# A 15-product matmul kernel: transposes in strict order with buffers per row, another product scheme, and divided block sums

## The chip, the cores and the metric

The kernel runs on one core of one Trainium2 chip. The metric is the device time of one execution in microseconds (us); lower is better. A run that is over 1.5% above the fastest run of the same kernel is called slow.

The engines are named as the profile names them: PE is TensorE, PEld its weight loads, DVE is VectorE, ACT is ScalarE, POOL is GpSimd, and SPq is the queue of SyncE, which here issues transposes, stores, weight loads and the first four x loads.

## The reference

```python
def setup_inputs():
    batch, m, k, n = 16, 512, 1024, 768
    return {"x": randn(batch, m, k), "w1": randn(k, n), "w2": randn(k, n)}   # float32

def reference(x, w1, w2):
    y1 = np.matmul(x, w1)
    y2 = np.matmul(x, w2)
    return (np.tanh(y1) * y2).astype(np.float32)
```

The 8192 rows of x are 64 row tiles of 128.

## The kernel before

Tiles 0 to 5 (the head) and tile 63 (the tail) are multiplied plainly. The 57 between form 19 triples. A triple is a block product of 3 row tiles x 2 halves of K with 2 halves of K x 3 column blocks. It would need 18 block products; a bilinear scheme does it in 15. Left operands are sums of x blocks (`A_SUMS`, ten small adds per triple, on VectorE or GpSimd), right operands are sums of weight blocks, made once (`B_SUMS`). Results are put together by letting products accumulate in PSUM banks, with copies and adds between them (`C_OPS`): "p" is a product of 4 matmuls of 128 x 512, "copy" and "seed" are ScalarE copies, "add" is VectorE, "t"/"th" are tanh of a full or half width, "m"/"mh" the multiplies by the second result. Names that begin with c are PSUM banks, those with s are SBUF tiles. In the cuts below, ... marks what is left out, and the comments behind # are mine.

```python
C_OPS = (
    ...
    ("p6", "p", (), "c1", 15, 40, True),
    ("add263", "add", ("copy327", "p6"), "c2", "c1", "s327", (-1, 1)),
    ("p12", "p", ("add263",), "c2", 47, 44, False),
    ...
    ("add16", "add", ("copy63", "p4"), "s16", "c6", "s63", (1, 1)),      # to SBUF
    ("m1", "m", ("add16", "t1"), 1, "s16", 1),                           # multiply: two SBUF inputs
    ...
    ("add38", "add", ("add128", "add16", "copy39", "p4"), "c6", "c6", "s39", (-1, 1)),
    ("p5", "p", ("add128", "add16", "add38"), "c6", 13, 43, False),
    ...
    ("add32", "add", ("copy7", "p0"), "s32", "c6", "s7", (1, 1)),        # to SBUF
    ("th1", "th", ("add32",), 1, "s32", 1),
    ("mh1", "mh", ("add32", "th1"), 1, "s32", 1),                        # half multiply: two SBUF inputs
)
PE_ORDER = "10 4+ 7 2+ 6 9 13+ 12 8 5+ 11 3 1+ 0+ 14+"     # "+": done in the next triple's period
```

The program is laid out by a list scheduler on the host (`Planner`). It is given each operation's engines, duration and dependencies ("needs" and "behind" become waits on the chip, "issued" is order in the program only), picks an engine and a place for each, and the instructions are then emitted in that order. Each engine's list keeps that order, and a wait in it holds up what stands behind: in the trace of the kernel before, VectorE sat 2.23 us at one sum with an add behind it that TensorE was waiting for (253.48 us, in the prediction). So a number in the planner changes no instruction's speed, but can change what stands behind what. A row tile comes in as follows:

```python
def load_x(e, mt):                       # GpSimd issues; f32 in HBM becomes f16 in SBUF
    xhs[mt] = xhpool.tile([P, K], f16, tag="xh", name="xh")
    pin(nc.gpsimd.dma_start(xhs[mt], xf[mt]))

def transpose(e, mt):                    # the SyncE queue issues
    xts[mt] = xtpool.tile([P, KO, P], f16, tag="xT", name="xT")
    pin(nc.sync.dma_start_transpose(xts[mt], xhs[mt]))
...
    op(f"L{mt}", {"pool": 0.55}, None, [], load_x, mt, issued=[prev] + ..., behind=..., xfer=1.38)
    op(f"T{mt}", {"sp": 0.05}, None, [f"L{mt}"], transpose, mt,
       behind=xt_readers[mt - XT_BUFS] if mt >= XT_BUFS else [], xfer=1.2)
```

## Time and profile before

| | before |
|---|---|
| median of the three runs ahead of the prediction | 335.29 us (334.16 to 336.82) |
| the profiled run | 339.59 us, span of the profile 337.8 us |
| work of the 19 triples at full pace | 19 x 60 matmuls x 0.2158 = 246.0 us |

The profiled run was slower than all three timed ones, 1.6% over the fastest. From the page of the kernel before, the busy shares and two rows of the span in 40 slices (a digit is the busy share in tenths, for PEclk the granted clock):

```profile
PE 299.8 (89%) x1394; PEld 138.1 (41%) x1394; DVE 246.9 (73%) x407; ACT 216.3 (64%) x430; POOL 149.2 (44%) x161
...
PE   7799949996999999999898898979797879899992
...
PEclk9999996997999999999999999999999999999998
```

The row of PE shows a dip in slice 6 and one in slice 10 (counted from 1), the clock falls in slices 7 and 10, and the pattern is broken from slice 20 on.

To compare kernels I use one figure throughout: in a stretch that holds only 128 x 512 matmuls, time lost = its length - (number of matmuls) x 0.2158 us. The count comes from the view of busy time by stretches. For the kernel before, 40 us from 90 hold 187 matmuls (nothing lost), and 150 us from 130 hold 599, so 150 - 129.3 = 20.7 us are lost.

### The profile page before, as it was taken

How to read it: one execution, taken by the hardware profiler on the slowest of the kernel's cores; microseconds unless marked ns; L12 is line 12 of the kernel's file. 1: busy time of each engine (PE TensorE's matmuls, PEld its weight loads, DVE VectorE, ACT ScalarE, POOL GpSimd, SP SyncE). 2: the span in 40 equal slices, each digit the busy share in tenths (PEclk: the TensorE clock that was granted, in tenths of full speed). 3: DMA queues.
4: the chain of work that ended last, by engine and by line, in shares of the span. 5: the costliest groups of instructions: out<-in, count | busy, mean ns of one | idle time of the engine just before them, and what ended most of it. 6: DMA issues, size and time to landing. Idle time of an engine off the chain costs nothing.

```text
span 337.8 us, 4563 instructions
## 1 busy us (share of the span) xinstructions
PE 299.8 (89%) x1394; PEld 138.1 (41%) x1394; DVE 246.9 (73%) x407; ACT 216.3 (64%) x430; POOL 149.2 (44%) x161
## 2 busy tenths in 40 slices
PE   7799949996999999999898898979797879899992
PEld 5456413442444444434343343434343334344440
DVE  0349997979679787887768687767768588898562
ACT  4595945884898876756676564757575565854531
POOL 2003274484367363663827365462718175451000
PEclk9999996997999999999999999999999999999998
DMA  8999999979999999799897999989897979533034
GB/s 266 340 406 192 194 171 322 230 124 217 185 218 245 155 228 230 129 230 134 223 197 163 210 143 241 108 222 121 232 157 186 172 169 265 98 142 140 0 143 188
DMA packets 84122, 65.33 MB, mean 193 GB/s; under 512 B 65664, under 2 KB 65664, under 8 KB 84096
## 3 DMA queue, kind: packets, MB, share of 16 engines
q1 hardware_dynamic: 74880, 47.72, 58.1%
q0 software_dynamic: 8640, 15.73, 30.5%
q10 hardware_dynamic: 576, 1.57, 1.2%
q8 instruction: 11, 0.18, 0.3%
q14 instruction: 15, 0.12, 0.1%
HBM read 39.85 MB, written 25.17 MB: 192 GB/s over the span
## 4 chain that ended last, share of the span: by engine, by line

## 5 line engine op out<-in xcount | busy, mean ns | idle before, releaser
L421 PE MATMUL bank<-b,s 128*128 128x512 f16 x608 | 144.8, 382 | 26.9 <-DVE bank L436 18.9
L421 PEld LDWEIGHTS <-s 128*128 128x128 f16 x760 | 74.9, 99 | 122.4 <-issue 37.3
L439 ACT ACTIVATE o<-s 128x512 f32<-128x512 f32 (+1 forms) x57 | 31.8, 558 | 68.7 <-DVE s L436 68.7
L380 POOL TENSOR_TENSOR s<-xT,s 128x512 f16<-128x512 f16 x37 | 43.0, 1164 | 64.1 <-PE bank L421 61.9
L380 POOL TENSOR_TENSOR s<-xT 128x512 f16<-128x512 f16 x35 | 42.3, 1226 | 53.6 <-DMA xT<-xh 28.0
L336 ACT ACTIVATE junk<-xh 128x1024 f16<-128x1024 f16 x60 | 63.1, 1052 | 0.9 <-DMA xh<-in_x_dram 0.7
L427 ACT ACTIVATE s<-bank 128x512 f32<-128x512 f32 x95 | 55.9, 589 | 9.5 <-PE bank L421 9.5
L421 PEld LDWEIGHTS <-xT 128*128 128x128 f16 x380 | 37.2, 98 | 45.3 <-issue 0.8
L436 DVE TENSOR_TENSOR bank<-s,bank 128x512 f32<-128x512 f32 x76 | 52.2, 687 | 4.3 <-PE bank L421 3.6
L444 DVE TENSOR_TENSOR o<-o,bank 128x512 f32<-128x512 f32 (+1 forms) x76 | 40.3, 548 | 17.6 <-PE bank L421 11.2
L421 PE MATMUL bank<-b,xT 128*128 128x512 f16 x228 | 52.5, 379 | 0.0
L436 DVE TENSOR_TENSOR s<-bank,s 128x512 f32<-128x512 f32 x57 | 38.8, 685 | 5.0 <-PE bank L421 3.5
L394 PE MATMUL bank<-wh,xT 128*128 128x512 f16 (+1 forms) x200 | 39.3, 353 | 1.3 <-DVE wh L312 0.7
L421 PE MATMUL bank<-wh,s 128*128 128x512 f16 x152 | 39.9, 386 | 0.0
L421 PE MATMUL bank<-wh,xT 128*128 128x512 f16 x152 | 38.8, 379 | 0.0
L329 POOL DMA_DIRECT2D xh<-in_x_dram x60 | 33.7, 563 | 7.4 <-DMA xT<-xh 3.9
L444 DVE TENSOR_TENSOR o<-o,s 128x512 f32<-128x512 f32 (+1 forms) x38 | 35.5, 934 | 0.5 <-ACT o L439 0.5
L439 ACT ACTIVATE o<-bank 128x256 f32<-128x256 f32 (+1 forms) x57 | 24.2, 453 | 17.0 <-DVE s L436 11.0
L380 DVE TENSOR_TENSOR s<-xT 128x512 f16<-128x512 f16 x22 | 16.4, 747 | 21.2 <-DMA xT<-xh 16.2
L380 POOL TENSOR_TENSOR s<-s,xT 128x512 f16<-128x512 f16 x19 | 27.6, 1453 | 8.8 <-DVE s L380 8.8
L380 DVE TENSOR_TENSOR s<-s,xT 128x512 f16<-128x512 f16 x38 | 20.4, 536 | 11.8 <-PE bank L421 10.4
L394 PEld LDWEIGHTS <-xT 128*128 128x128 f16 x200 | 19.6, 99 | 19.5 <-issue 2.1
(41 smaller groups left out, 149.0 us busy)
## 6 DMA issues: line engine op xcount, KB each, us to landing
out_dram<-o SPq DMA_DIRECT2D x63, 384.0 KB, 3.6
xh<-in_x_dram POOLq DMA_DIRECT2D x60, 256.0 KB, 5.6
w_f<-in_w_dram SPq DMA_DIRECT2D x12, 384.0 KB, 9.0
x_f<-in_x_dram SPq DMA_DIRECT2D x4, 512.0 KB, 8.2
w_f<-in_w_dram ACTq DMA_DIRECT2D x4, 384.0 KB, 9.1
xT<-xh SPq DMA_TRANSPOSE x60, 5.8
out_dram<-o_last SPq DMA_DIRECT2D x1, 384.0 KB, 4.7
```

The lines of the kernel that those rows point to most:

```text
L329: pin(nc.gpsimd.dma_start(xhs[mt], xf[mt]))
L336: pin(nc.scalar.activation(junk[:, :src.shape[-1]], src, ACT.Abs, scale=scale, accum_out=sums[:, column:column + 1]))
L380: pin(engine[e].tensor_tensor(ss[i, v], x_operand(i, a), x_operand(i, b), OP[how]))
L394: pin(nc.tensor.matmul(b, xts[mt][:, k, :], rhs, start=first, stop=k == KO - 1, skip_group_check=True))
L421: pin(nc.tensor.matmul(place(i, dst), x_operand(i, a)[:, k, :], w_rhs(b, k), start=begins and k == 0, stop=k == KH - 1, skip_group_check=T ...
L427: pin(nc.scalar.activation(d, place(i, src), ACT.Copy, scale=float(sign)))
L436: pin(nc.vector.tensor_tensor(d, a, b, ALU.add if signs == (1, 1) else ALU.subtract))
L439: pin(nc.scalar.activation(out_tile(HEAD + 3 * i + r)[:, lo:lo + n], place(i, src)[:, :n], ACT.Tanh, scale=float(sign)))
L444: pin(nc.vector.tensor_tensor(o, o, place(i, src)[:, at:at + n], ALU.mult))
```

## The change

The intent, in five parts: (1) each transpose is issued only after the one of the row tile ahead of it, and transposed tiles get four buffers for each of a triple's three rows (12, were 10 in one ring), with more xh (6, were 5) and output buffers (4 of each, were 3) and longer transpose latencies in the planner; (2) another 15-product scheme in which every multiply reads its second result from a PSUM bank, and so does every tanh but two per triple; (3) with it, another order of the products; (4) a fixed division of x block sums, five on GpSimd and five on VectorE; (5) at the start, GpSimd's x loads wait for a weight slice (the gate, empty before), and the head's stores go later. Two planner entries of the check at the end (f1, f4) changed as well.

```diff
-    (5, 1, 4, "add"), (13, 5, 8, "add"), (20, 16, 4, "sub"), ...
+    (10, 2, 8, "sub"), (3, 1, 2, "add"), (34, 32, 2, "sub"), ...
+ON_POOL = (34, 35, 51, 10, 21)
 ...                                   (B_SUMS and C_OPS replaced; some lines of the new C_OPS:)
+    ("p6", "p", (), "c3", 15, 5, True),
+    ("add312", "add", ("copy376", "p6"), "c5", "c3", "s376", (1, 1)),
+    ("p9", "p", ("add312",), "c5", 31, 37, False),
+    ("add2", "add", ("copy63", "p1"), "c2", "c1", "s63", (1, 1)),
+    ("m0", "m", ("add2", "t0"), 0, "c2", 1),
+    ("add4", "add", ("copy56", "p3"), "c8", "c1", "s56", (-1, 1)),
+    ("th0", "th", ("add4",), 0, "c8", 1),
+    ("mh0", "mh", ("add4", "th0"), 0, "c8", 1),
 ...
-PE_ORDER = "10 4+ 7 2+ 6 9 13+ 12 8 5+ 11 3 1+ 0+ 14+"
+PE_ORDER = "7 0+ 13+ 6 10 4+ 5+ 9 12 1 14 3+ 2+ 11 8"
 ...                                   (planner: an operation may name its own latency; slack of 1.0 for transfers "behind")
-    XH_BUFS, XT_BUFS, S_BUFS, O_BUFS, C_BUFS, WF_BUFS = 5, 10, 2, 3, 2, 8
+    XH_BUFS, XT_BUFS, S_BUFS, O_BUFS, C_BUFS, WF_BUFS = 6, 4, 2, 4, 2, 8
-        xts[mt] = xtpool.tile([P, KO, P], f16, tag="xT", name="xT")
+        xts[mt] = xtpool.tile([P, KO, P], f16, tag=f"xT{mt % 3}", name="xT")
-    def nothing(e):
-        pass
+    def gate(e):
+        pin(nc.gpsimd.tensor_copy(held, wfs[1, GATE][:, :1]))
-            op(f"S{v}.{i}", {"dve": 0.416, "pool": 1.2}, ...
+            op(f"S{v}.{i}", {"pool": 1.25} if v in ON_POOL else {"dve": 0.45}, ...
-           issued=[f"T{HEAD + 5}"] if mt < HEAD else [], xfer=1.0)
+           issued=[f"T{HEAD + 8 + mt // 3 * 3}"] if mt < HEAD else [], xfer=1.0)
         op(f"T{mt}", {"sp": 0.05}, None, [f"L{mt}"], transpose, mt,
-           behind=xt_readers[mt - XT_BUFS] if mt >= XT_BUFS else [], xfer=1.2)
+           issued=[f"T{mt - 1}"] if mt > 4 else [],
+           behind=xt_readers[mt - 3 * XT_BUFS] if mt >= 3 * XT_BUFS else [], xfer=1.2, latency=3.0)
```

More of the change, by code (lines that the diff above doesn't have):

```diff
@@ L15 @@
 A_SUMS = (
-    (5, 1, 4, "add"), (13, 5, 8, "add"), (20, 16, 4, "sub"), (12, 4, 8, "add"), (28, 12, 16, "sub"),
-    (15, 2, 13, "add"), (60, 32, 28, "sub"), (47, 15, 32, "sub"), (42, 47, 5, "sub"), (63, 16, 47, "sub"),
+    (10, 2, 8, "sub"), (3, 1, 2, "add"), (34, 32, 2, "sub"), (35, 34, 1, "sub"), (11, 3, 8, "sub"),
+    (51, 16, 35, "add"), (15, 11, 4, "sub"), (31, 16, 15, "sub"), (63, 31, 32, "add"), (21, 10, 31, "add"),
 )
 B_SUMS = (
-    (48, 32, 16, "sub"), (40, 8, 32, "sub"), (3, 1, 2, "sub"), (6, 2, 4, "sub"), (43, 3, 40, "sub"),
@@ L21 @@
-    (44, 4, 40, "add"), (45, 6, 43, "add"), (18, 16, 2, "sub"), (19, 1, 18, "add"), (36, 44, 8, "sub"),
-    (27, 8, 19, "sub"),
+    (48, 32, 16, "sub"), (5, 1, 4, "add"), (36, 32, 4, "sub"), (6, 4, 2, "sub"), (37, 1, 36, "sub"),
+    (24, 8, 16, "add"), (45, 37, 8, "sub"), (18, 16, 2, "sub"), (29, 5, 24, "sub"), (27, 29, 6, "sub"),
+    (26, 2, 24, "sub"),
 )
+ON_POOL = (34, 35, 51, 10, 21)
 C_OPS = (
     ("p10", "p", (), "c0", 32, 8, True),
-    ("copy327", "copy", ("p10",), "s327", "c0", 1),
@@ L31 @@
-    ("p6", "p", (), "c1", 15, 40, True),
-    ("add263", "add", ("copy327", "p6"), "c2", "c1", "s327", (-1, 1)),
-    ("p12", "p", ("add263",), "c2", 47, 44, False),
-    ("seed7", "seed", ("p12",), "c3", "c2", -1),
-    ("p11", "p", ("seed7",), "c3", 42, 36, False),
-    ("copy7", "copy", ("p11",), "s7", "c3", -1),
-    ("p7", "p", (), "c4", 16, 1, True),
-    ("p4", "p", (), "c6", 12, 3, True),
-    ("add64", "add", ("copy327", "p7"), "s64", "c4", "s327", (1, 1)),
-    ("t2", "t", ("add64",), 2, "s64", 1),
@@ L41 @@
-    ("p14", "p", ("p12", "seed7"), "c2", 63, 4, False),
-    ("th2", "th", ("p14",), 2, "c2", 1),
-    ("mh2", "mh", ("p14", "th2"), 2, "c2", 1),
-    ("p9", "p", ("add64", "p7"), "c4", 28, 19, False),
-    ("copy191", "copy", ("p9",), "s191", "c4", 1),
-    ("p8", "p", ("copy191", "p9"), "c4", 20, 18, False),
-    ("copy63", "copy", ("p8",), "s63", "c4", -1),
-    ("p3", "p", ("copy63", "p8"), "c4", 8, 27, False),
-    ("add39", "add", ("copy7", "p3"), "c5", "c4", "s7", (-1, 1)),
-    ("p2", "p", ("add39",), "c5", 5, 45, False),
@@ L51 @@
-    ("copy39", "copy", ("p2",), "s39", "c5", -1),
-    ("add1", "add", ("add263", "copy39", "p6"), "s1", "c1", "s39", (-1, 1)),
-    ("t0", "t", ("add1",), 0, "s1", 1),
-    ("t1", "t", ("p3",), 1, "c4", -1),
-    ("add16", "add", ("copy63", "p4"), "s16", "c6", "s63", (1, 1)),
-    ("m1", "m", ("add16", "t1"), 1, "s16", 1),
-    ("add128", "add", ("copy191", "p4"), "c8", "c6", "s191", (-1, 1)),
-    ("p13", "p", ("add128",), "c8", 60, 16, False),
-    ("m2", "m", ("p13", "t2"), 2, "c8", 1),
-    ("add38", "add", ("add128", "add16", "copy39", "p4"), "c6", "c6", "s39", (-1, 1)),
@@ L61 @@
-    ("p5", "p", ("add128", "add16", "add38"), "c6", 13, 43, False),
-    ("seed2", "seed", ("p5",), "c7", "c6", 1),
-    ("p1", "p", ("seed2",), "c7", 2, 48, False),
-    ("m0", "m", ("p1", "t0"), 0, "c7", 1),
-    ("p0", "p", ("p5", "seed2"), "c6", 1, 6, False),
-    ("th0", "th", ("p0",), 0, "c6", 1),
-    ("mh0", "mh", ("p0", "th0"), 0, "c6", 1),
-    ("add32", "add", ("copy7", "p0"), "s32", "c6", "s7", (1, 1)),
-    ("th1", "th", ("add32",), 1, "s32", 1),
-    ("mh1", "mh", ("add32", "th1"), 1, "s32", 1),
+    ("p1", "p", (), "c1", 3, 24, True),
@@ new lines @@
+    ("p6", "p", (), "c3", 15, 5, True),
+    ("p7", "p", (), "c4", 16, 1, True),
+    ("copy376", "copy", ("p7",), "s376", "c4", -1),
+    ("add312", "add", ("copy376", "p6"), "c5", "c3", "s376", (1, 1)),
+    ("p9", "p", ("add312",), "c5", 31, 37, False),
+    ("seed56", "seed", ("p9",), "c6", "c5", 1),
+    ("p8", "p", ("seed56",), "c6", 21, 36, False),
+    ("copy56", "copy", ("p8",), "s56", "c6", -1),
+    ("add64", "add", ("copy376", "p10"), "s64", "c0", "s376", (-1, 1)),
+    ("t2", "t", ("add64",), 2, "s64", -1),
@@ new lines @@
+    ("p14", "p", ("p9", "seed56"), "c5", 63, 32, False),
+    ("th2", "th", ("p14",), 2, "c5", 1),
+    ("mh2", "mh", ("p14", "th2"), 2, "c5", 1),
+    ("p12", "p", ("add64", "p10"), "c0", 35, 26, False),
+    ("copy191", "copy", ("p12",), "s191", "c0", -1),
+    ("p11", "p", ("copy191", "p12"), "c0", 34, 18, False),
+    ("copy63", "copy", ("p11",), "s63", "c0", -1),
+    ("p0", "p", ("copy63", "p11"), "c0", 1, 27, False),
+    ("t0", "t", ("p0",), 0, "c0", 1),
+    ("add2", "add", ("copy63", "p1"), "c2", "c1", "s63", (1, 1)),
@@ new lines @@
+    ("m0", "m", ("add2", "t0"), 0, "c2", 1),
+    ("add60", "add", ("copy56", "p0"), "c7", "c0", "s56", (1, -1)),
+    ("p4", "p", ("add60",), "c7", 10, 45, False),
+    ("copy60", "copy", ("p4",), "s60", "c7", -1),
+    ("add8", "add", ("copy60", "p6"), "s8", "c3", "s60", (1, 1)),
+    ("t1", "t", ("add8",), 1, "s8", 1),
+    ("add128", "add", ("copy191", "p1"), "c10", "c1", "s191", (1, 1)),
+    ("p13", "p", ("add128",), "c10", 51, 2, False),
+    ("m2", "m", ("p13", "t2"), 2, "c10", 1),
+    ("p5", "p", ("add128", "add2", "p1"), "c1", 11, 29, False),
@@ new lines @@
+    ("add52", "add", ("add128", "add2", "copy60", "p5"), "c1", "c1", "s60", (1, 1)),
+    ("seed16", "seed", ("add52",), "c9", "c1", -1),
+    ("p2", "p", ("seed16",), "c9", 4, 6, False),
+    ("m1", "m", ("p2", "t1"), 1, "c9", 1),
+    ("p3", "p", ("add52", "seed16"), "c1", 8, 48, False),
+    ("add4", "add", ("copy56", "p3"), "c8", "c1", "s56", (-1, 1)),
+    ("th0", "th", ("add4",), 0, "c8", 1),
+    ("mh0", "mh", ("add4", "th0"), 0, "c8", 1),
+    ("th1", "th", ("p3",), 1, "c1", 1),
+    ("mh1", "mh", ("p3", "th1"), 1, "c1", 1),
@@ L86, in __init__, with op @@
         self.next = {}
-    def op(self, name, engines, due, needs, fn, *args, behind=(), issued=(), chains=(), xfer=0.0, seeds=False):
+    def op(self, name, engines, due, needs, fn, *args, behind=(), issued=(), chains=(), xfer=0.0, latency=None, seeds=False):
         assert name not in self.ops, name
         self.ops[name] = dict(engines=engines, due=due, needs=[n for n in needs if n], behind=[n for n in behind if n], issued=[n for n in issued if n], fn=fn, args=args,
-                              chains=chains, xfer=xfer, seeds=seeds)
+                              chains=chains, xfer=xfer, latency=latency, seeds=seeds)
         for c in chains:
@@ L188, in run @@
                 bandwidth = max(bandwidth, f) + o["xfer"]
-                done = bandwidth + self.LATENCY["cast" if e == "pool" else "sp"]
+                done = bandwidth + (o["latency"] or self.LATENCY["cast" if e == "pool" else "sp"])
             else:
@@ L210, in run @@
                 same = e in ("act", "dve", "pe") and e in self.ops[u]["engines"]
-                ready_at[u] = max(ready_at[u], done + (0.05 if same else 0.0 if o["xfer"] else self.LATENCY[e]))
+                slack = 1.0 if n in self.ops[u]["behind"] and self.ops[u]["xfer"] else 0.0
+                ready_at[u] = max(ready_at[u], done + slack + (0.05 if same else 0.0 if o["xfer"] else self.LATENCY[e]))
                 left[u] -= 1
@@ L250 @@
     LOW, HIGH = 512.0, 1024.0
-    XH_BUFS, XT_BUFS, S_BUFS, O_BUFS, C_BUFS, WF_BUFS = 5, 10, 2, 3, 2, 8
+    XH_BUFS, XT_BUFS, S_BUFS, O_BUFS, C_BUFS, WF_BUFS = 6, 4, 2, 4, 2, 8
     WARM = 21
     AHEAD = 3
+    GATE = 2
     FILL = (-10, -6, -4)
@@ L276 @@
     count = once.tile([P, 1], bf16, name="count")
+    held = once.tile([P, 1], f32, name="held")
     junk = once.tile([P, K], f16, name="junk")
@@ L331, in transpose @@
     def transpose(e, mt):
-        xts[mt] = xtpool.tile([P, KO, P], f16, tag="xT", name="xT")
+        xts[mt] = xtpool.tile([P, KO, P], f16, tag=f"xT{mt % 3}", name="xT")
         pin(nc.sync.dma_start_transpose(xts[mt], xhs[mt]))
@@ L561 @@
                 finals(mt, 1, "M", ("M", mt, 0), base + 1.7 * (n + 1) + 3, last, at=G)
-    op("gate", {"pool": 0.1}, 20.5, ["Lb2"], nothing)
+    op("gate", {"pool": 0.1}, 20.5, [f"Lb{GATE}"], gate)
     c_ops = {o[0]: o for o in C_OPS}
@@ L605 @@
         for v, a, b, how in A_SUMS:
-            op(f"S{v}.{i}", {"dve": 0.416, "pool": 1.2}, None, x_needs(i, a) + x_needs(i, b), x_sum, i, v, a, b, how,
+            op(f"S{v}.{i}", {"pool": 1.25} if v in ON_POOL else {"dve": 0.45}, None, x_needs(i, a) + x_needs(i, b), x_sum, i, v, a, b, how,
                behind=[f"{r}.{i - S_BUFS}" for r in a_readers[v]] if i >= S_BUFS else [])
@@ L652 @@
         op(f"T{mt}", {"sp": 0.05}, None, [f"L{mt}"], transpose, mt,
-           behind=xt_readers[mt - XT_BUFS] if mt >= XT_BUFS else [], xfer=1.2)
+           issued=[f"T{mt - 1}"] if mt > 4 else [],
+           behind=xt_readers[mt - 3 * XT_BUFS] if mt >= 3 * XT_BUFS else [], xfer=1.2, latency=3.0)
         op(f"D{mt}", {"act": 1.25}, ORIGIN - 12 + 4.33 * (mt - HEAD), [f"L{mt}"], abs_x, mt)
-    op("f1", {"dve": 0.2}, None, [], flag_1, behind=[f"D{mt}" for mt in range(MT)] + [f"aw{a}{k}" for a, t, k in slices])
+    op("f1", {"dve": 0.3}, None, [], flag_1, behind=[f"D{mt}" for mt in range(MT)] + [f"aw{a}{k}" for a, t, k in slices])
     op("f2", {"dve": 0.2}, None, ["f1"], flag_2)
     op("f3", {"dve": 0.2}, None, ["f2"], flag_3)
-    op("f4", {"pe": 0.3}, ORIGIN, ["f3"], flag_4, chains=["flag"])
+    op("f4", {"pe": 0.3}, ORIGIN, [], flag_4, behind=["f3"], chains=["flag"])
     op("f5", {"dve": 0.2}, ORIGIN + 15 * SLOT * TRIPLES - 10, ["f4"], flag_5, chains=["flag"])
```

## The prediction

> **What bounds the kernel now.** I read the busy shares first (TensorE 89%, VectorE 73%, ScalarE 64%, GpSimd 44%, DMA nearly full until 300 us), then TensorE in order of time, because a busy share says nothing about pipelined matmuls. (The chain that ended last is empty on this page, so the path has to be put together from the timelines.) The work is 19 triples of row tiles, each 15 products of 4 matmuls. Where nothing stalls, one triple takes 12.95 us (the run of 12 matmuls on `b,xT` starts at 86.34, 99.29, 112.24 and 125.19), that is 60 matmuls at 0.2158 us. From 125.19 to 303.50 there are 12 triples, which would be 155.4 us at that pace; they take 178.3. So 22.9 us are lost there, always at the same two places. From the timeline of TensorE (start, us, engine, line, operation, in brackets the idle time before it and what ended it):
>
> ```profile
> 252.87 1.03 PE L421 MATMUL bank<-wh,s 128*128 128x512 f16 x4
> 255.16 1.89 PE L421 MATMUL bank<-b,s 128*128 128x512 f16 x8 [1.26 <-DVE bank L436]
> 257.83 1.89 PE L421 MATMUL bank<-b,s 128*128 128x512 f16 x8 [0.78 <-DVE bank L436]
> 259.55 2.75 PE L421 MATMUL bank<-b,xT 128*128 128x512 f16 x12
> ```
>
> The stall of 1.26 is p12 waiting for add263; the one of 0.78 is p5 of the triple before, waiting for add38. (A matmul's end is modelled 0.17 us late, so each stall is worth that much more.) What VectorE did meanwhile, from the timeline of all engines:
>
> ```profile
> 253.48 0.42 DVE L380 TENSOR_TENSOR s<-xT 128x512 f16<-128x512 f16 x1 [2.23 <-DMA xT<-xh]
> 253.53 2.49 POOL L380 TENSOR_TENSOR s<-xT 128x512 f16<-128x512 f16 x2 [4.44 <-DMA xT<-xh]
> ...
> 254.42 0.69 DVE L436 TENSOR_TENSOR bank<-s,bank 128x512 f32<-128x512 f32 x1
> 255.02 1.56 DVE L444 TENSOR_TENSOR o<-o,s 128x512 f32<-128x512 f32 x1
> ...
> 256.50 0.67 DVE L436 TENSOR_TENSOR s<-s,bank 128x512 f32<-128x512 f32 x1
> 257.10 0.68 DVE L436 TENSOR_TENSOR bank<-s,bank 128x512 f32<-128x512 f32 x1
> ```
>
> VectorE works in program order. It sat 2.23 us at an x block sum whose transposed tile had not landed; add263 (254.42) stood behind it. Then one multiply with both inputs in SBUF took 1.56 us, and add38 (257.10) stood behind that. Why the tile was late stands in the timelines of the DMA queue and of GpSimd:
>
> ```profile
> 228.20 1.11 POOL L329 DMA_DIRECT2D xh<-in_x_dram  x2
> ...
> 242.22 0.58 POOL L329 DMA_DIRECT2D xh<-in_x_dram  x1
> ```
>
> ```profile
> 237.16 2.40 SPq L333 DMA_TRANSPOSE xT<-xh  x1
> ...
> 245.89 5.48 SPq L333 DMA_TRANSPOSE xT<-xh  x2
> ```
>
> The second of the loads at 228.20 landed at 234.7. A transpose is issued at 237.16, the next only at 245.89: the queue's wait before it names the semaphore of the load issued at 242.22, which needed 3.6 us. So the queue stands some 6 us at the transpose of a tile of the NEXT triple, and the last row tile of this triple, 11 us in SBUF, goes behind it at 247.29 and lands at 253.4, where both sums start. The load at 242.22 in turn stood on GpSimd behind sums that waited for the previous late tile. It is a loop of one turn per triple, and it repeats from 134 us on.
>
> The other loss is at the start of the triples. From 42.9 to 86.3 there are 144 matmuls, 31.1 us of work in 43.4: 12.3 us lost, in one stall of 5.08 (to 51.18) and one of 2.90 (to 79.48), each followed by a stretch at half clock (49.1 to 55.9 and 79.8 to 83.2, costing some 2.4 and 1.7). The second one:
>
> ```profile
> 73.44 4.79 DVE L444 TENSOR_TENSOR o<-o,s 128x256 f32<-128x256 f32 x1
> ...
> 74.58 2.26 POOL L380 TENSOR_TENSOR s<-xT 128x512 f16<-128x512 f16 x2
> ...
> 79.48 1.57 PE L421 MATMUL bank<-b,s 128*128 128x512 f16 x4 [2.90 <-DVE s L436]
> ```
>
> A half multiply, usually 0.42 us, took 4.79 beside four GpSimd sums in a row. The first stall has an x block sum of 4.59 us in the same position.
>
> **What the Trainium skill says.** "SBUF — State Buffer", section "Who interferes with whom": a VectorE instruction with two SBUF inputs takes the read interface it shares with GpSimd, and whichever comes second is blocked wholly; one with at most one SBUF input isn't. The trace agrees:
>
> ```profile
> L444 DVE TENSOR_TENSOR o<-o,bank 128x512 f32<-128x512 f32 x38 | 25.9, 681 | 11.3 <-PE bank L421 11.2
> ...
> L444 DVE TENSOR_TENSOR o<-o,s 128x512 f32<-128x512 f32 x19 | 22.8, 1200 | 0.0
> ...
> L444 DVE TENSOR_TENSOR o<-o,bank 128x256 f32<-128x256 f32 x38 | 14.5, 415 | 6.3 <-ACT o L439 6.3
> ...
> L444 DVE TENSOR_TENSOR o<-o,s 128x256 f32<-128x256 f32 x19 | 12.7, 667 | 0.5 <-ACT o L439 0.5
> ```
>
> "TensorE: Matmul & The Clock Gate", section "HAM oscillation", puts a return to half clock on idle gaps of more than about 3.4 us; here it followed gaps of 5.08 and already of 2.90 us, and none of 2.2 or less. "Perfetto Trace Analysis", section "Identifying the Most-Contended Engine", warns of DMA occupancy as a bound; here a share of 1.06 was sustained from 80 to 120 us at the full pace of 12.95 us per triple, so I take the nearly full DMA for no bound.
>
> **The change, part by part.**
> 1. Strict transposes, four buffers for each row of a triple (12, were 10 in one ring), six xh buffers (were 5), an assumed transpose latency of 3.0 us (was 1.6; measured 5.8 from issue). The held-back tile could go at 239.6, directly after the one at 237.16, and land near 245, 8 us earlier; the loop is cut. Gain: the p12 stalls. Eight are listed from 163 to 271 us, 0.72 to 2.18, sum 10.2, with 0.17 for each 11.6.
> 2. tanh products read banks. 38 multiplies leave the SBUF form: 19 x (1.200 - 0.681) + 19 x (0.667 - 0.415) = 9.9 + 4.8 = 14.7 us of VectorE, 0.77 per triple. Off the path in itself, but the p5 stall lies behind one such multiply: 1.56 falls to 0.68, which takes 0.88 off a stall of 0.79 + 0.17. 11 stalls: 10.5 us. The 4.79 us event cannot recur in this form (worth 2.9 + 1.7). Instruction counts stay: 5 copies, 2 seeds, 8 adds, 15 products, 12 tanh and multiplies.
> 3. The slack of the scheme. Between p6 and the product that needs its sum there were 2 product slots of 0.863 us (add263), now 3 (add312 before p9); add64 before its product 2 before, 3 now. ScalarE keeps hops of 2 slots (seed56, copy63), in which a copy of 0.59 fits, as before. Against it: accumulators live longer. Summing lifetimes in slots by hand I get about 90 of 120 bank slots before and 99 now, with all 8 banks taken near slot 5 and slot 13.
> 4. Sums divided for good: GpSimd 5 per triple (were 91 in all, now 95) at 1.16 to 1.45, about 6.2 us plus 1.7 for issuing 3 loads, of 12.95; VectorE 5 at some 0.54. No engine is over its time: VectorE 8 x 0.685 + 3 x 0.681 + 3 x 0.415 + 2.7 = 11.5 of 12.95, ScalarE as before. Neutral.
> 5. Start: the gate now really waits for a weight, so three x loads issued at 1.44 no longer compete with the weights; T4 waits longer in turn. The head's stores go later, out of the way of the transposes (five stores held the queue from 45.8 to 49.9). I count 0 for the gate and 8 of the 12.3 us for the start, since x block sums on VectorE remain in the blockable form.
>
> Sum: steady 22.9, of which I credit 20, plus 8, less 2 for new bank waits: 26. 335.3 - 26 = 309.
>
> **The rivals.** (a) DMA becomes the bound: its packet time is 303 us of the span. Uncontended (22 ns for a 256 B transpose packet, the lowest I see) a triple needs about 12.1 us of 12.95, so it fits only just; for it, the share over 0.9; against it, the sustained full pace from 80 to 134 us. If true, a triple settles near 14 us: time about 320. (b) Bank waits: 8 of 8 banks in use twice a period; one wait of 0.5 us per triple gives 10 us, time about 318. (c) The shared port: x sums on VectorE starved by GpSimd runs, as in the 4.59 us event; if every triple loses 1 us, 325. (d) Everything works: 42.9 head + 246.0 + 5.5 tail products + 6.5 to the end, plus about 0 for the offset of span and time: near 300.
>
> **Range and chances.** The loss is measured and both causes are removed by construction, so faster is very likely; how much is open between (d) and (b) or (c). 309, range 299 to 325. Faster 0.91, same 0.06, slower 0.03.
>
> **What would show it.** Part 1: transposes in row order, no wait of 6 us of the DMA queue at a load with another tile ready; no `DVE s <- DMA xT<-xh` waits. Part 2: no `o<-o,s` multiplies, all at 0.68 and 0.42. Start: no half clock between 45 and 85. A wrong prediction would show as periods over 13.5 us with another releaser: ScalarE copies or seeds (banks), sums of several us (port), or transposes landing late although issued early (DMA).

## More of the kernel before

Where the first product on a weight sum starts, from the timeline of TensorE:

```profile
44.63 1.03 PE L421 MATMUL bank<-b,s 128*128 128x512 f16 x4
```

## The result, and the profile after

| | runs, us | state |
|---|---|---|
| before, same rounds | 334.16, 335.29, 336.82, 336.75 | fast |
| changed | 314.64, 315.31 | fast |
| changed | 323.14, 338.76 | slow |

A ratio here is of one kernel's fast runs to the other's in the same rounds. It isn't the ratio of the medians, and it can differ by up to a point from the quotient of the means of all fast runs (a_nogate below: 0.948, quotient 0.939; b_sch_str_div: 0.937, quotient 0.944). For the changed kernel it is 0.938, with a 95% interval from 0.931 to 0.946: faster by 6%. The median of all four runs is 319.23, because two of four were slow; one of them, 338.76, is above every run of the kernel before in the same rounds. The profile is of a fast run.

The changed kernel's page, the same rows as before:

```profile
PE 296.1 (95%) x1394; PEld 137.9 (44%) x1394; DVE 239.9 (77%) x406; ACT 218.0 (70%) x430; POOL 146.6 (47%) x163
...
PE   8999596999998999989999999999999999999993
...
PEclk9999798899999999999999999999999999999999
```

From slice 8 on, PE is at 8 or 9 tenths in every slice but the last. What is left is a dip in slice 5 and one in slice 7, each with a fall of the clock. From the timeline of TensorE, the two stalls at the start, the first product on a weight sum (47.71), and one period of the steady part:

```profile
35.01 12.00 PE L399 MATMUL bank<-wh,xT 128*128 128x512 f16 x47 [3.60 <-DMA xT<-xh]
...
47.71 1.03 PE L426 MATMUL bank<-b,s 128*128 128x512 f16 x4
...
52.79 4.44 PE L426 MATMUL bank<-b,s 128*128 128x512 f16 x12 [2.98 <-DVE bank L441]
...
223.10 4.48 PE L426 MATMUL bank<-b,s 128*128 128x512 f16 x20
227.42 1.03 PE L426 MATMUL bank<-wh,s 128*128 128x512 f16 x4
...
236.05 4.48 PE L426 MATMUL bank<-b,s 128*128 128x512 f16 x20
```

Each group between 223.10 and 236.05 starts before the modelled end of the one ahead, so nothing is idle; the period is 12.95 us (223.10 to 236.05). The run of 20 matmuls on sums at 223.10 holds p9, the counterpart of the old p12, and p5, so it is the place that answers to the two stalls of before. From the view of what the SyncE queue waited for (us in total, times, longest), first before, then changed:

```profile
SPq L333 <- DMA xh<-in_x_dram: 85.9, 17, 7.8
```

```profile
SPq L338 <- PE bank L426: 77.1, 18, 6.4
...
SPq L338 <- DMA xh<-in_x_dram: 19.2, 10, 9.4
```

The transposes hardly stand at loads any more (19.2 us for 85.9; the longest, 9.4 us, is the first transpose, issued at 26.48 after the gate). They mostly wait for a free xT buffer, which is the wait of a queue that runs ahead. The multiplies, from the groups by shape:

```profile
L449 DVE TENSOR_TENSOR o<-o,bank 128x512 f32<-128x512 f32 x57 | 37.5, 681 | 2.6 <-ACT o L444 1.2
...
L449 DVE TENSOR_TENSOR o<-o,bank 128x256 f32<-128x256 f32 x57 | 22.8, 411 | 4.9 <-ACT o L444 4.9
```

All are at 681 and 411 ns, and the form with two SBUF inputs is gone. And from the busy time by stretches (columns: PE, PEld, DVE, ACT, POOL with counts, then granted clock, DMA share, GB/s), the steady part of the changed kernel:

```profile
86.00:280.00 194.00, 191.56 (x886) 86.33 (x885) 160.34 (x284) 143.41 (x285) 107.50 (x115) 1.00 1.06 209
```

886 matmuls are 191.2 us of work, 2.8 us lost in 194. The DMA share of 1.06 (the view can go over 1) is held for 194 us at full pace, so the transfers are not the bound (rival (a) of the prediction).

So the steady part is as hoped, but the page shows a cost that I had put at zero: the triples start later. The first product on a weight sum starts at 47.71 us, against 44.63 before.

### The profile page after: what moved, and what is told of

Same layout as the page of the kernel before. It is cut to its first block, busy times and chain, and to the rows that moved or that the text cites. A ratio compares the mean times of both kernels' runs of the same rounds, so it can differ in the third digit from the quotient of the medians.

```text
span 312.9 us, 4544 instructions
## 1 busy us (share of the span) xinstructions
PE 296.1 (95%) x1394; PEld 137.9 (44%) x1394; DVE 239.9 (77%) x406; ACT 218.0 (70%) x430; POOL 146.6 (47%) x163
## 4 chain that ended last, share of the span: by engine, by line
PE 47%; DMA 6%; issue 3%; POOL 1%; ACT 1%; DVE 1%; SPq 1%; POOLq 0%; ACTq 0%
PE bank L426 45%; DMA xh<-in_x_dram 4%; DMA out_dram<-o 2%; PE bank L399 2%; POOL s L385 1%; SPq L338 1%; DVE s L385 0%; ACT o L444 0%; ACT bank L432 0%; DVE bank L441 0%; DVE o_last L409 0%; ACT junk L341 0%; SPq L393 0%; ACT s L432 0%; PE bank L464 0%
## 5 line engine op out<-in xcount | busy, mean ns | idle before, releaser
L441 DVE TENSOR_TENSOR bank<-bank,s 128x512 f32<-128x512 f32 x95 | 65.8, 693 | 19.6 <-PE bank L426 10.5
L385 POOL TENSOR_TENSOR s<-xT 128x512 f16<-128x512 f16 x38 | 44.7, 1177 | 58.5 <-PE bank L426 52.4
L449 DVE TENSOR_TENSOR o<-o,bank 128x256 f32<-128x256 f32 (+1 forms) x114 | 59.1, 546 | 7.5 <-ACT o L444 6.1
L426 PE MATMUL bank<-b,xT 128*128 128x512 f16 x228 | 55.4, 379 | 0.0
L444 ACT ACTIVATE o<-bank 128x256 f32<-128x256 f32 x76 | 33.0, 436 | 25.2 <-DVE bank L441 17.2
L385 POOL TENSOR_TENSOR s<-s,s 128x512 f16<-128x512 f16 x19 | 22.9, 1208 | 36.7 <-DVE s L385 36.7
L385 DVE TENSOR_TENSOR s<-s,xT 128x512 f16<-128x512 f16 x57 | 35.0, 613 | 4.5 <-PE bank L426 4.3
L444 ACT ACTIVATE o<-s 128x512 f32<-128x512 f32 x38 | 23.7, 624 | 3.5 <-DVE s L441 3.5
L385 POOL TENSOR_TENSOR s<-xT,s 128x512 f16<-128x512 f16 x19 | 22.6, 1189 | 4.3 <-PE bank L426 4.3
L432 ACT ACTIVATE bank<-bank 128x512 f32<-128x512 f32 x38 | 20.7, 573 | 4.9 <-PE bank L426 3.9
L385 POOL TENSOR_TENSOR s<-s,xT 128x512 f16<-128x512 f16 x19 | 22.4, 1179 | 0.6
```

The costliest lines, as they stand in the source:

```text
L385: pin(engine[e].tensor_tensor(ss[i, v], x_operand(i, a), x_operand(i, b), OP[how]))
L426: pin(nc.tensor.matmul(place(i, dst), x_operand(i, a)[:, k, :], w_rhs(b, k), start=begins and k == 0, stop=k == KH - 1, skip_group_check=T ...
L432: pin(nc.scalar.activation(d, place(i, src), ACT.Copy, scale=float(sign)))
L441: pin(nc.vector.tensor_tensor(d, a, b, ALU.add if signs == (1, 1) else ALU.subtract))
L444: pin(nc.scalar.activation(out_tile(HEAD + 3 * i + r)[:, lo:lo + n], place(i, src)[:, :n], ACT.Tanh, scale=float(sign)))
L449: pin(nc.vector.tensor_tensor(o, o, place(i, src)[:, at:at + n], ALU.mult))
```

## The experiments

Any edit makes the planner lay out the whole program anew. No experiment here is a change of one instruction with all others in place. All twelve gave right results. Times are fast runs unless marked; each job ran on one chip with its own runs of the kernel before. "Lost" is the figure defined above, for the two stretches.

| kernel | fast runs, us | slow runs | ratio to before (95%) | lost 90 to 130 | lost 130 to 280 |
|---|---|---|---|---|---|
| before (profile of a slow run) | 334.2 to 336.8 (328.8 to 336.8 over all jobs) | | 1 | 0 | 20.7 |
| changed | 314.6, 315.3 | 2 | 0.938 (0.931 to 0.946) | 0.9 | 1.5 |
| b_strict | 319.4 to 323.1 (4) | 0 | 0.961 (0.953 to 0.969) | 4.4 | 0 |
| b_order_bufs | 325.5 to 329.7 (4) | 0 | 0.980 (0.972 to 0.989) | 5.9 | 5.0 |
| b_scheme | 314.8 to 316.2 (3) | 1 | 0.941 (0.933 to 0.949) | 4.6 | 0.9 |
| a_nogate | 313.9, 315.3 | 2 | 0.948 (0.938 to 0.959) | 0.3 | 0.7 |
| a_sbufmul | 315.1 to 316.0 (3) | 1 | 0.948 (0.941 to 0.955) | 3.5 | 0.9 |
| a_notstrict (profile of a slow run) | 319.2 to 320.5 (3) | 2 | 0.960 (0.953 to 0.968) | not compared | not compared |
| a_flexsums | 315.9, 320.5 | 2 | unclear | 2.7 | 5.2 |
| a_gate_a7 | 323.8, 324.6 | 2 | unclear | 1.6 | 8.7 |
| b_bank | 328.9, 331.5 | 2 | unclear | 3.5 | 15.3 |
| b_strict_bank | 318.1 to 321.8 (4) | 0 | 0.956 (0.942 to 0.971) | 2.0 | 1.7 |
| b_sch_str_div | 312.4 to 313.8 (4) | 0 | 0.937 (0.925 to 0.949) | 0.7 | 0 |
| b_ssd_stores | 311.1 to 314.5 (4) | 2 | 0.937 (0.930 to 0.944) | 0.9 | 0 |

The recorded verdict (2%) is "faster" for the changed kernel, b_strict, b_scheme, a_nogate and b_ssd_stores, and "unclear" for the other eight, also where the interval lies below 0.98 (a_sbufmul, a_notstrict, b_strict_bank, b_sch_str_div). In the jobs of these four, three of eight and four of seven runs of the kernel before were slow, so their ratios are less firm than the intervals look. The traces carry more of what follows than the ratios do. The 20.7 us of the kernel before come from a slow run; a fast run of it took some 4 us less, and no trace of one was kept.

My theory was the prediction's: the order of the transposes removes the stall of p12, the bank multiplies remove that of p5 and one event at the start, and the gains add up. The main rivals were that the scheme does it alone, and that order needs the new buffers to act.

### b_strict: the kernel before with strict order alone

```diff
         op(f"T{mt}", {"sp": 0.05}, None, [f"L{mt}"], transpose, mt,
+           issued=[f"T{mt - 1}"] if mt > 4 else [],
```

> The kernel before, with one thing of the change: each transpose is issued after the one of the row tile ahead of it. My theory (the queue stands at a later tile's load while a landed tile waits behind it): the stalls of p12 go (11.6 us of the 22.9 lost from 125 to 303 us), the 0.79 us stalls of p5 stay because the multiply with two SBUF inputs stays; about 324 us. Rival A (the new scheme's slack does it all, order is nothing): 335. Rival B (order without the new buffers only moves the wait to the buffer that is not free): 330 or more, with the queue waiting for TensorE instead.

One clause gives 3.9%, and both of rivals A and B fall. But more went than I had said: from 130 to 280 us nothing is lost at all. The p5 stalls went with the p12 stalls, and the slow multiply stayed, as the groups by shape of this run show:

```profile
L444 DVE TENSOR_TENSOR o<-o,s 128x512 f32<-128x512 f32 x19 | 21.5, 1132 | 0.0
```

1132 ns against 1200 before. So the slow multiply by itself stalls nothing; the p5 stall also needs a VectorE that is late. What remains in this run lies ahead of 130 us. Between 90 and 130 the stall of p12 is there three times, 1.28 us each, without a late tile: VectorE is late because an x block sum that usually takes 0.42 us took 2.52, 2.58 and 2.58 us beside GpSimd sums. From the timelines of VectorE and TensorE, the first of the three:

```profile
92.63 2.52 DVE L380 TENSOR_TENSOR s<-xT 128x512 f16<-128x512 f16 x1 [0.16 <-PE bank L421]
...
96.41 3.71 PE L421 MATMUL bank<-b,s 128*128 128x512 f16 x16 [1.28 <-DVE bank L436]
```

So p12 has two causes, the late tile and a blocked sum; why the second ends after 126 us stays open. The largest event is at 70 us. The timeline of all engines there:

```profile
70.32 1.17 POOL L380 TENSOR_TENSOR s<-s,s 128x512 f16<-128x512 f16 x1
70.55 6.23 DVE L444 TENSOR_TENSOR o<-o,s 128x256 f32<-128x256 f32 x1
...
72.02 1.17 POOL L380 TENSOR_TENSOR s<-xT,s 128x512 f16<-128x512 f16 x1
73.13 2.25 POOL L380 TENSOR_TENSOR s<-xT 128x512 f16<-128x512 f16 x2
75.34 1.14 POOL L380 TENSOR_TENSOR s<-s,xT 128x512 f16<-128x512 f16 x1
...
78.03 1.44 PE L421 MATMUL bank<-b,s 128*128 128x512 f16 x3 [5.26 <-DVE s L436]
```

A half multiply took 6.23 us, from just after the first GpSimd sum began to the end of the fifth. It is the event of the kernel before at 73.44, and larger.

The planner's list of transposes also corrects a detail of my prediction. The tile that was held back before is row 1 of a triple, not the last row: the order before was row 2, row 0 of the next triple, row 1. The wait and its cause are as I read them.

### b_order_bufs: the changed kernel with the old scheme

```diff
-A_SUMS, B_SUMS, C_OPS, PE_ORDER of the changed kernel
+A_SUMS, B_SUMS, C_OPS, PE_ORDER of the kernel before
-            op(f"S{v}.{i}", {"pool": 1.25} if v in ON_POOL else {"dve": 0.45}, ...
+            op(f"S{v}.{i}", {"dve": 0.416, "pool": 1.2}, ...
```

> The changed kernel with the old 15-product scheme and the old undivided sums: order, buffers, gate, store times and planner figures are the new ones. My theory: p5 stalls of 0.79 us stay (11 to 17 of them), p12 stalls are gone, the start is as in the changed kernel: about 324 to 326. Rival A (scheme alone): 335. Rival B (buffers needed for the order to act): clearly below the run with strict order alone, by 5 us or more.

The size was about right and the reason only in part. The time is about 6 us worse than with strict order alone, the opposite of rival B: the other parts of (1) and (5) cost the old scheme time. Part of this is the start, where the first product on a weight sum is at 48.23 us (44.49 in b_strict); the steady part has small stalls of 0.18 us in a period of 13.37 us (140.51 to 153.88). Which of the other parts costs the time is not separated.

### b_scheme: the kernel before with the new scheme alone

```diff
-A_SUMS, B_SUMS, C_OPS, PE_ORDER of the kernel before
+A_SUMS, B_SUMS, C_OPS, PE_ORDER of the changed kernel
```

> The kernel before with the new scheme and its order of products, nothing else: sums undivided, transposes free, 10 shared buffers. My theory: no multiply with two SBUF inputs, so the p5 stalls (10.5 us) and the second early stall (4.6 us) go; late tiles remain where a transpose is issued out of order: about 321. Rival A (scheme does it all): 312 to 316.

Rival A's number came in: 314.8 to 316.2, as good as the whole change. The planner of this kernel, run on the host, gives the transposes as row 1, row 0 of the next triple, row 2. So one still stands behind a tile of the next triple, but the loads of these last two are issued back to back (two at 216.34 us on GpSimd), and the SyncE queue waits for x loads only 4.5 us in all (85.9 before). In the kernel before, row 1 stood behind row 0 of the next triple, whose load was issued only after the late sums. So the loop of the kernel before belonged to the places that the old scheme and the free order give together, and either strict order or the new scheme breaks it. The two gains (13 and 20 us, means of fast runs) overlap and don't add up.

### a_nogate: the changed kernel with an empty gate

```diff
     def gate(e):
-        pin(nc.gpsimd.tensor_copy(held, wfs[1, GATE][:, :1]))
+        pass
```

> The changed kernel with the gate empty again, as before: the x loads of tiles 4 to 9 are issued at 1.4 us and compete with the weights. My theory after the result: in the changed kernel the gate let tile 4 land only at 34.96, which cost a stall of 3.6 us and half clock after it (1.7 us); without the gate the weights come some 3 us later but TensorE doesn't stand at tile 4: 311 to 313. Rival (the weights' early arrival is worth as much): 315 to 316, no difference.

The mechanism held and the gain did not appear: 313.9 and 315.3. Tile 4 lands at 30.0 instead of 34.96, and the stall of 3.60 us there is gone, but the next stall has grown from 2.98 to 5.81 us:

```profile
53.65 4.20 PE L426 MATMUL bank<-b,s 128*128 128x512 f16 x12 [5.81 <-DVE bank L441]
```

### a_sbufmul: the changed kernel with two multiplies per triple from SBUF again

```diff
-    ("add2", "add", ("copy63", "p1"), "c2", "c1", "s63", (1, 1)),
-    ("m0", "m", ("add2", "t0"), 0, "c2", 1),
+    ("add2", "add", ("copy63", "p1"), "s2", "c1", "s63", (1, 1)),
+    ("m0", "m", ("add2", "t0"), 0, "s2", 1),
 (and add4, th0, mh0 from "c8" to "s4")
```

> The changed kernel with one full and one half multiply per triple put back into the form with both inputs in SBUF (add2 and add4 write SBUF tiles in place of banks), all else as it is. My prediction's reading (such a multiply costs 0.77 us of VectorE per triple and stalls p5-like products by 0.8 to 1 us each triple): 315 + 10 to 15 = 325 to 330, VectorE some 10 to 15 us busier. Rival, after the run with strict order alone, where these multiplies stayed slow (1132 ns) and the stalls were gone all the same: VectorE gets busier, but the time stays within 3 us of the changed kernel, 312 to 318.

The rival's number came in. The fast runs are 315.1 to 316.0, the steady part loses 0.9 us. The multiplies did get slower, by the groups by shape:

```profile
L449 DVE TENSOR_TENSOR o<-o,s 128x512 f32<-128x512 f32 x19 | 14.8, 780 | 0.2
L449 DVE TENSOR_TENSOR o<-o,s 128x256 f32<-128x256 f32 x19 | 14.0, 736 | 0.0
```

They cost 19 x (0.780 - 0.681) + 19 x (0.736 - 0.411) = 8.1 us of VectorE, off the path. VectorE is 9.6 us busier in all (249.5 for 239.9), which the reading had forecast, and the time did not follow. A single stall behind such a multiply shows (2.21 us at 100). The ratio is a point worse than the changed kernel's, with intervals that overlap and different jobs, so a per cent can't be excluded; the 3 to 5% of my reading can.

### a_notstrict: the changed kernel without strict order

```diff
-           issued=[f"T{mt - 1}"] if mt > 4 else [],
```

> The changed kernel without the clause that keeps transposes in order; new scheme, divided sums and buffers stay. If order matters whatever the scheme (my prediction's part 1): a wait per triple comes back, 322 or more. Rival, after the run with the new scheme alone: with the new scheme the planner gives no transpose a place behind a later load anyway, so 313 to 317.

Between the two: fast runs 319.2 to 320.5, some 5 us above the changed kernel's. a_sbufmul, timed in the same job, is at 315.1 to 316.0. So strict order is worth something with the new buffers and divided sums too, and b_scheme doesn't need it. The rival's premise was wrong for this kernel: from tile 32 on its planner gives row 0, row 2, row 1, so that row 1 stands behind a later load in every triple. The profile fell on a slow run, so I don't say from it where the 5 us are; its SyncE queue waits 57.9 us for x loads (19.2 in the changed kernel), which fits but proves nothing.

### a_flexsums: the changed kernel with undivided sums

```diff
-            op(f"S{v}.{i}", {"pool": 1.25} if v in ON_POOL else {"dve": 0.45}, ...
+            op(f"S{v}.{i}", {"dve": 0.45, "pool": 1.25}, ...
```

> The changed kernel with its x block sums undivided (either engine, as the planner finds it free). If the division is neutral, as predicted: 313 to 317. Rival: undivided sums pile on GpSimd in runs and lock out VectorE, 318 to 325.

Inconclusive in time: 315.9 and 320.5 with two slow runs. The profile is of the run of 320.5; it loses 5.2 us in the steady part, in stalls of 2.37, 1.73 and 0.62 us between 147 and 181, each behind ScalarE. I had called the division neutral; that can't be upheld or refuted with two fast runs.

### a_gate_a7: the gate on an earlier slice

```diff
-        pin(nc.gpsimd.tensor_copy(held, wfs[1, GATE][:, :1]))
+        pin(nc.gpsimd.tensor_copy(held, wfs[0, 7][:, :1]))
-    op("gate", {"pool": 0.1}, 20.5, [f"Lb{GATE}"], gate)
+    op("gate", {"pool": 0.1}, 17.0, ["La7"], gate)
```

> The changed kernel with the gate on the last slice of the first weight in place of the third slice of the second, some 3 to 4 us earlier. If the stall of 3.6 us at tile 4 and the 1.7 us of half clock after it are the gate's doing: tile 4 lands by 32, both go, 310 to 312. Rival: the earlier loads take DMA from the weights and the stall comes back as waits for weights, or the gain is lost at the first triples as without a gate (8.0 us lost there instead of 5.4): 313 to 316.

Both expectations failed; it is worse, 323.8 and 324.6. The x loads went out 4.6 us earlier (16.51 for 21.08), but each transfer took longer: the load of tile 4 took 7.65 us to land (5.38 in the changed kernel) and its transpose 11.92 (8.48). Tile 4 landed at 36.1, later than before the edit, and TensorE stood longer:

```profile
36.14 12.51 PE L399 MATMUL bank<-wh,xT 128*128 128x512 f16 x47 [4.37 <-DMA xT<-xh]
```

With no gate the first three x loads are done by 17 us, and their transposes go at 20.9. I read this as x loads and transposes against the rest of the weights at once; the longer times to landing fit, but no run separates it. Why the steady part of this kernel loses 8.7 us as well stays open.

### b_bank: the kernel before with bank multiplies alone

```diff
-    ("add16", "add", ("copy63", "p4"), "s16", "c6", "s63", (1, 1)),
-    ("m1", "m", ("add16", "t1"), 1, "s16", 1),
+    ("add16", "add", ("copy63", "p4"), "c9", "c6", "s63", (1, 1)),
+    ("m1", "m", ("add16", "t1"), 1, "c9", 1),
 (and add32, th1, mh1 from "s32" to "c10")
```

> The kernel before (old scheme, free order) with only the multiplies changed: add16 and add32 write banks, so every tanh product is a multiply from a bank. My prediction's step (p5 stalls are the slow multiply's, 10.5 us, and the early event of 4.79 us with its half clock, 4.6): 335 - 15 = 320, p12 stalls stay. Theory now (in the steady part both stalls follow from the late tile; only the early event is the shared port's): the stalls near 0.8 or more per triple stay, the early event goes: 328 to 332.

The theory's number came in (328.9 and 331.5, with two slow runs; the verdict is unclear), but it was half right. The stall of p5 did go: each period now has one stall, where the kernel before had two. From the timeline of TensorE, two periods:

```profile
203.46 3.68 PE L421 MATMUL bank<-b,s 128*128 128x512 f16 x16 [1.31 <-DVE bank L436]
217.52 3.68 PE L421 MATMUL bank<-b,s 128*128 128x512 f16 x16 [0.89 <-DVE bank L436]
```

All 16 matmuls now run through where there was a break of 0.78 after 8. But the period is 14.06 us here, and 15.3 us are still lost from 130 to 280: the p5 stall was 10.5 us in 11 triples by the prediction's working, and 20.7 - 15.3 = 5.4 us were gained. It would be rash to say that half of it came back at p12. One event, a stall of 3.39 us at p12 (to 234.08, behind a tile that kept VectorE waiting 4.36 us) and the 3.4 us at half clock after it, makes some 5.3 of the 15.3 us. What is firm: the loop of load, transpose and sums is still there, and the time shows no clear gain (the fast runs mean 330.2, those of the kernel before in the same job 331.5).

### b_strict_bank: the kernel before with strict order and bank multiplies

The edits of b_strict and of b_bank together.

> The kernel before with strict order and bank multiplies, still the old scheme. In the run with strict order alone a half multiply with two SBUF inputs took 6.23 us at 70.5 beside four GpSimd sums, then came a stall of 5.26 us and 6.8 us at half clock. Theory: that event goes, some 8 us: 313 to 316, as good as the whole change, so the scheme's longer slack is worth little. Rival (the gain of the new scheme is its slack): 320 to 323.

The event at 70 us is gone, and the gain is less than half of what I expected: 318.1 to 321.8, 2.5 us under b_strict in the means, from another job. In its place the first stall is there, with 4.63 us and 6.8 us of half clock, behind an x block sum on VectorE that took 4.60 us at 44.37, the one of 4.59 us that the kernel before has in that place. x block sums have two SBUF inputs in every scheme. So part of the new scheme's advantage at the start isn't the bank multiplies. Whether it is its slack or the places of its sums is not separated by these runs.

### b_sch_str_div: new scheme, strict order, divided sums, nothing else

```diff
 (the kernel before, with the new scheme of b_scheme, the clause of b_strict, and)
-            op(f"S{v}.{i}", {"dve": 0.416, "pool": 1.2}, ...
+            op(f"S{v}.{i}", {"pool": 1.25} if v in ON_POOL else {"dve": 0.45}, ...
```

> New scheme, strict order and divided sums, but the gate, the times of the head's stores, the planner's figures and all buffer counts of the kernel before. The start of the triples should be at 43 to 44 as before (the changed kernel: 47), and the steady part without stalls. If the first triples lose no more than in the changed kernel (5.4 us to 90 us): 310 to 312, better than both. Rival (as without a gate: the early gain is lost again at the first triples): 314 to 316.

All four runs are fast, 312.4 to 313.8, between the two expectations. The triples start at 44.47, the steady part loses nothing, and one large stall remains:

```profile
52.15 4.07 PE L423 MATMUL bank<-b,s 128*128 128x512 f16 x12 [4.05 <-DVE bank L438]
```

The new buffer counts, the gate and the planner's latencies are not needed for these times.

### b_ssd_stores: the same with the head's stores later

```diff
-           issued=[f"T{HEAD + 5}"] if mt < HEAD else [], xfer=1.0)
+           issued=[f"T{HEAD + 8 + mt // 3 * 3}"] if mt < HEAD else [], xfer=1.0)
```

> The best so far (new scheme, strict order, divided sums, everything else of before) with one more part of the change: the head's stores go later. In the best so far five of them hold the DMA queue from 45.3 to 49.2 while the tile for the next transpose has landed at 45.4, and TensorE stalls 4.05 us to 52.15. If those stores are the cause: that stall falls by 2 us or more, the loss up to 90 us from 6.9 to 4 or less, 309 to 311. Rival (the stall is VectorE's, behind two weight sums of 2.2 and 1.2 us and blocked x sums): no change, 312 to 314.

The time came out near the lower number (three of the fast runs at 311.1 to 311.6, one at 314.5, two slow ones), the reason did not. The stall is still there, with 4.27 us, so it isn't the stores' (none is issued between 36.8 and 51.3 us), and 5.7 us are lost up to 90 us. The timeline shows VectorE busy ahead of it:

```profile
47.71 2.16 DVE L372 TENSOR_TENSOR b<-b,wh 128x2048 f16<-128x2048 f16 x1
...
49.80 1.37 DVE L382 TENSOR_TENSOR s<-xT 128x512 f16<-128x512 f16 x1
51.08 0.69 DVE L438 TENSOR_TENSOR bank<-bank,s 128x512 f32<-128x512 f32 x1
...
51.82 1.44 PE L423 MATMUL bank<-b,s 128*128 128x512 f16 x3 [4.27 <-DVE bank L438]
```

The add at 51.08 stands behind a weight sum of 2.16 us (1.21 when nothing is in its way) and an x sum of 1.37 (0.42). Both have two SBUF inputs, and GpSimd sums run beside them. No run takes these sums away, so that they cause the stall is read from the trace and not shown by an experiment.

This version is faster than the kernel before; b_sch_str_div is unclear, with an interval well below 1. Against the changed kernel they are 2 to 3 us faster in the means of fast runs, but they were not run in the same rounds, and the ratios (0.937 and 0.938) don't tell them apart.

## Why the prediction was right or wrong

The direction was right, and the fast runs at 315 lie inside the range, some 6 us from 309. That the median, 319.23, lies close to the numbers of rivals (a) and (b) is chance: it is raised by two slow runs, and the trace has neither a period near 14 us nor a bank wait in every triple. By its steps:

**The loop of the late tile (part 1): right.** b_strict shows it alone. The term was mis-sized: I credited 11.6 us of steady loss to it, and strict order alone removes all of the steady loss (20.7 us from 130 to 280 on the page of before, 0 in b_strict). What I had not seen is that the new scheme alone breaks the loop as well (b_scheme).

**The p5 stalls as the slow multiply's (part 2, 10.5 us): wrong as a term of a sum.** This step failed: "the p5 stall lies behind one such multiply: 1.56 falls to 0.68, which takes 0.88 off a stall of 0.79 + 0.17. 11 stalls: 10.5 us". The stall needs a late VectorE and a slow multiply; taking away either ends it (b_strict, b_bank). While the loop stands, the gain in time is not clear of noise (b_bank). Once the loop is cut, the multiply's form is worth about a per cent at most (a_sbufmul). In the sum it did no harm, and that is luck: the wrong split of the two stalls had the right total.

**The event at the start in the multiply: right in kind.** It recurs with 6.23 us in b_strict and is gone in b_strict_bank. In the other place a blocked x sum of 4.60 us stayed, as I had allowed. My sign "no half clock between 45 and 85" failed: 3.4 us from 52.9 follow the stall of 2.98 us, with a weight sum of 2.17 us on VectorE (49.62) ahead of it beside GpSimd sums.

**The gate at zero: it held in the net, but not by its steps.** I had said only that tile 4 waits longer. In fact the first product on a weight sum starts 3.1 us later (47.71 for 44.63), with a stall of 3.60 us at tile 4 and 3.4 us of half clock from 35.9. Both are absent in a_nogate, and its time is the same all the same (313.9 and 315.3): what is saved at tile 4 returns at the next stall. In the kernels with the buffers of before and no gate, the start is at 43.7 to 44.7.

**The start of the triples, 8 of 12.3: nearly right.** From its first product on a weight sum to 90 us the changed kernel loses 5.4 by the figure of above, so 6.9 were gained.

**Bank waits, 2 us: right in size.** From 90 to 280 us the changed kernel has three stalls of TensorE, of 1.10, 0.85 and 0.49 us (100.45, 135.99, 214.47), each behind ScalarE, 2.4 us in all; none comes with every triple.

**Taking the loss from a slower run: wrong.** I took 26 us, read from a profile of a run of 339.6, off a median of 335.3. From the two pages, 337.8 - 312.9 = 24.9 us were gained, close to 26; in fast runs it is 335.8 - 315.0 = 20.8 (means). So of the 5.7 us between 309.3 and 315.0, 4.3 are the base (339.6 - 335.3) and 1.1 the sum. That the sum came so close is luck in part: of the 24.9, the start gave 6.9 (8 credited), the later start took 3.1 (0 credited), and so the rest gave 21.1, where I had credited 20 - 2 = 18.

**The clock's return to half:** "none of 2.2 or less" holds for the trace that I read, but not beyond it: in b_scheme half clock followed a stall of 2.09 us (last section).

**The division as neutral:** left open (a_flexsums). What makes some runs of the changed kernel slow, 323 and 339 us, is open too. I explain nothing by them. I only note that two of the four timed runs of each of the changed kernel, a_nogate, a_flexsums, a_gate_a7 and b_bank were slow, and none of b_strict, b_order_bufs, b_strict_bank and b_sch_str_div, of four each.

## What to carry to other kernels

When several waits repeat with one period, look for the loop that sets the period before adding up the waits: here one clause that kept a ready transpose from standing behind a load not yet issued removed both stalls from 130 us on, while removing the other wait alone gave no gain clear of noise (b_bank). What counts on an in-order queue is when the thing waited for is issued: b_scheme keeps a transpose behind one of the next triple and loses 0.9 us, because both loads go out together. Take a loss from a profile only in relation to the time of the very run that was profiled, and test a start-up guard by itself: here the gate's wait was paid for at tile 4, and taking it out was paid for at the next stall.

## What the Trainium skill lacked or had wrong

- DMA: Bandwidth & Descriptors, section "Issuing engines are not separate DMA queues": it weighs the issuing engine by the time to initiate a DMA alone, "usually small relative to the DMA itself". What it lacks is the order on one issuing queue, where a DMA that waits for its semaphore holds up ready ones behind it: here a wait of 6.25 us at one transpose (from 239.6 us in the kernel before) with a landed tile behind it, and 3.9% of the time for one clause (b_strict).
- SBUF — State Buffer, section "Who interferes with whom": the instruction that comes second is said to be blocked until the first finishes. Here a multiply with two SBUF inputs stayed blocked through a whole run of GpSimd sums with a DMA issue between them: 6.23 us for an instruction that takes 0.41 from a bank (b_strict), 4.79 before. In other places the wait was far shorter (780 ns on average for the full width in a_sbufmul, 681 from a bank).
- TensorE: Matmul & The Clock Gate, section "HAM oscillation — how this bites in real kernels": it warns of idle gaps of more than about 3.4 us. Here 3.4 us at half clock followed stalls of 2.90 us (before), 2.98 (changed), 2.45 (b_order_bufs, to 120.35) and 2.09 (b_scheme, to 49.39), and did not follow stalls of 3.38 (a_gate_a7, to 141.17) and 3.04 (b_bank, to 93.66). So in these traces the length of the gap alone does not decide. The length of the stretches (3.4 or 6.8 us) agrees with the window that the section gives.
